# Layer 0 attention of a two-layer encoder: gate and reciprocal loads on POOL's queue, wider steps, a copied block of meta columns, and a shared PSUM bank read by ScalarE

## The chip, the cores and the metric

The kernel runs on one core of a Trainium2 chip. The core has TensorE (PE in the profile; PEld is its weight load), VectorE (DVE), ScalarE (ACT), GpSimd (POOL) and SyncE (SP), which issues most of the DMAs; POOL issues DMAs too. Each engine, and each queue of DMA issues, works in the order in which the program lists its instructions. The metric is the device time of one execution in microseconds (us), lower is better. Before the change it is 1822.5 us, the median of three runs (1821.57 to 1823.12).

## The reference

Two layers work on 512 tokens, with 16 learned meta tokens put in front, of width 2048. Layer 0 is softmax attention, layer 1 gated linear attention. Each layer is wrapped in two RMS norms and a residual. The change touches layer 0 and one helper that both layers use. What layer 0 computes:

```python
proj = h @ w_in                      # q 16 heads, k and v 8 heads of 128, gate 16 x 128
q = axial_rope(rmsnorm(q, q_norm)); k = axial_rope(rmsnorm(k, k_norm))
s = q @ k.T * 128 ** -0.5            # per head; two query heads share a k and a v
p = softmax(s)
o = p @ v
y = (o * silu(gate)) @ w_out
```

## The kernel before

All activations lie with features on the partitions and the 528 tokens along the free axis (512 real tokens, then the 16 meta tokens). Every product is made of three: each operand is split into a high part of fewer bits and the rest, and high x high, high x low and low x high are added in PSUM (`three`, lines 154 to 156; the weights' split is a cast on ACT, line 131, and a subtraction on DVE, line 132). A projection of 128 output features (`project`) is 2 halves x 16 blocks x 3 matmuls of 264 columns.

**How the order is made.** The text of the kernel is traced in the order of a small planner, `Clock`. It counts the time of projections (each triple of matmuls adds 3 x 271/2400 us) and lets generators take turns: a generator that yields 5.0 goes on when 5.0 us of projections have been laid down. The traced order is only a priority. The program's scheduler then lays out each engine's list, and may put an instruction of lower priority earlier, if it thinks the engine free and the operands ready. Weights are traced with a higher priority, so that their loads run ahead.

**Gates and values.** The gate projections of heads 0 to 12 and the v projections come first, in pairs of 128 features by a scheme of seven half-size products in place of eight (`seven`). Two outputs y1 and y2 are put together from partial sums. Some sums stay in PSUM: bank `p1` is read, and then the next product is added on top. Its third reading gave y2's right half, by an add on DVE straight from PSUM (line 249); two products later the bank is added to again. `seven` is called 18 times: 8 in layer 0's input, 4 in its output, 6 in layer 1's input. The gates lie in DRAM (`g_d`) until they are used.

**Attention.** The loop over the 8 groups (one k and v head, two query heads) runs three things at once. The three projections for the next group's k and q are PE's steady work. `attention` goes over 9 query tiles of the present group, one per step of `SLOTS` (2.9 us, 3.2 in the last group): scores in the one PSUM buffer `s` (two banks, lines 683 to 685), row maximum on DVE (688), exp with row sum on ACT (691), a second exp that writes the meta columns twice more into the tail of `pn` (693), the reciprocal of the row sum (695 or 697); half a step later the tile is transposed on PE (703, 705) and split (707 to 710), and the product with v follows (723 to 726). The next tile's scores can only start when line 693 has read `s`. At a group's end `inverses` stores the reciprocals of the row sums to DRAM (`r_d`).

`stored_gates` is the third: for the two heads of the group before, it loads the gates (line 655, SP's queue, buffers `gr`, two), loads a head's reciprocals as a row on all partitions (`inverse`, line 637, SP's queue, buffer `rb`, one), multiplies the gate by the first norm's factor (660, DVE), takes its SiLU (139 to 141 on ACT, the product 671 on POOL, buffers `gs`, two), multiplies by the reciprocals (`divided`, 642 for 512 and 643 for 16 columns, POOL), multiplies the head's output (665, DVE) and stores it by POOL's queue (666). Heads 13 to 15 have their gates projected in place (`gate`) in the last group. `rope` turns q and k: four DMAs (312) and three operations (313 to 315) on POOL, behind the evacuation of the projection (305, 306), while a sum of squares on PE (326, 327) gives the norm (329, 333).

Of the kernel before, what the change touches and what calls it, by code (L numbers as in the profile page):

```python
# [10 lines left out]
F32 = mybir.dt.float32  # L11
F32R = mybir.dt.float32r
I32 = mybir.dt.int32
AF = mybir.ActivationFunctionType
# [5 lines left out]
P = 128  # L20
# [12 lines left out]
G_HEADS = 4  # L33
SCALE = 128 ** -0.5
AHEAD = 400
SLOTS = (2.9,) * 7 + (3.2,)


class Clock:
# [43 lines left out]
def hybrid_encoder(  # L83
# [132 lines left out]
    def seven(src, c, ys, th, tl, free, ps_x):  # L216
# [58 lines left out]
        A.copy(y2[:, r], p5)  # L275
        sums(a11, a12, a11)
        product(parts(a21), of_t(T3), p1, True)
        add(y2[:, r], p1, y2[:, r])
        product(parts(a11), of_u(1, 1), p5, True)
        add(y1[:, r], p5, y1[:, r])  # L280
        product(parts(a22), of_t(T4), p1, True)
# [350 lines left out]
            rope(qw, sq, outs[i], (4.0, 8.8, 9.8))  # L632
        return qk, vv

    def inverse(h):
        rb = wa.tile([P, T], F32, tag="rb", name="rb", bufs=1)
        nc.sync.dma_start(out=rb, in_=r_d[h // 2, h % 2:h % 2 + 1, :].broadcast_to([P, T]))
        return rb

    def divided(gs, rb):  # L640
        by = gs[:, :SEQ].rearrange("p (t q) -> p t q", t=4)
# [9 lines left out]
    def stored_gates(hs, held):  # L651

        grs = [wa.tile([P, T], F32, tag="gr", name="gr") for _ in hs]
        for gr, h in zip(grs, hs):
            nc.sync.dma_start(out=gr, in_=g_d[h])
        yield 6.0
        for gr, h in zip(grs, hs):
            rb = inverse(h)
            yield 5.0
            V.tensor_tensor(gr, gr, rrow, op=ALU.mult)  # L660
            gs = silu(gr)
            divided(gs, rb)
            yield 4.0
            og = held[h % 2]
            V.tensor_tensor(og, og, gs, op=ALU.mult)
            nc.gpsimd.dma_start(out=og_d[h], in_=og)

    def silu(gr):
        gs = wa.tile([P, T], F32, tag="gs", name="gs", bufs=2)
# [10 lines left out]
    def softmax(n, qh, ql, kh, kl, inv):  # L680
        s = ps_s.tile([P, 2, 512], F32, tag="s", name="s")[:n, :, :HALF]
        for i, (a, b) in enumerate(HALVES):
            PE.matmul(s[:, i], qh, kh[:, a:b], start=True, stop=False)  # L683
            PE.matmul(s[:, i], ql, kh[:, a:b], start=False, stop=False)
            PE.matmul(s[:, i], qh, kl[:, a:b], start=False, stop=True)  # L685
        mx = wa.tile([P, 1], F32, tag="mx", name="mx")[:n]
        sm = wa.tile([P, 1], F32, tag="sm", name="sm")[:n]
        V.reduce_max(mx, s, axis=AX.XY, negate=True)  # L688
        pn = pn_bufs[n_pn[0] % NP][:n]
        n_pn[0] += 1  # L690
        A.activation(pn[:, :T].rearrange("p (a b) -> p a b", a=2), s, AF.Exp, bias=mx, accum_out=sm)  # L691
        tail = pn[:, SEQ:].rearrange("p (r m) -> p r m", r=3)
        A.activation(tail[:, 1:, :META], s[:, 1, HALF - META:].unsqueeze(1).broadcast_to([n, 2, META]), AF.Exp, bias=mx)  # L693
        if inv is None:
            V.reciprocal(tail[:, ::2, META], sm.broadcast_to([n, 2]))
        else:
            V.reciprocal(inv[:n], sm)
        return pn
# [36 lines left out]
    def attention(g, qk, vv, o_sb, slot):  # L735
        qh, ql, kh, kl = qk
        q0 = (0, Q1)
        last = g == KV - 1
        rs = None if last else wa.tile([P, 9], F32, tag="rs", name="rs")
        early, late = [[[None], [None]] for _ in range(2)]  # L740

        def tile_of(a, t):
            cell, end = (late, 272) if t > 1 else (early, 256)
            t2 = t % 2
            done = t2 and not (t > 1 and a == 0)
            return (P, q0[a] + t * P, [(cell[a], 0, t2 * P, P)], [(cell[a], 256 * (t > 1), end, a)] if done else [],
                    [] if t2 else [cell[a]], a * 4 + t)
        todo = [tile_of(0, t) for t in range(4)]
        todo.append((2 * META, SEQ, [(late[a], a * META, 256, META) for a in range(2)], [(late[0], 256, 272, 0)],
                     [late[1]], 8))  # L750
        first = tile_of(1, 2)
        todo += [first[:4] + ([],) + first[5:], tile_of(1, 3), tile_of(1, 0), tile_of(1, 1)]
        prev = None
        for item in todo + [None]:
            if item is not None:
                n, c, puts, ends, fresh, i = item
                pn = softmax(n, qh[:, c:c + n], ql[:, c:c + n], kh, kl, None if last else rs[:, i:i + 1])
            yield slot / 2
            if prev is not None:
                n_, _, puts_, ends_, fresh_, _ = prev[0]  # L760
                for cell in fresh_:
                    cell[0] = p_tiles()
                transposed(prev[1], n_, [(cell[0], qc, cc, m) for cell, qc, cc, m in puts_])
                for cell, cc, m, a in ends_:
                    clk.after(slot * 1.1, lambda cell=cell, cc=cc, m=m, a=a:
                              weighted(cell[0], cc, m, vv, o_sb[a], last))
            yield slot / 2
            prev = (item, pn) if item is not None else None
        if not last:
            inverses(g, rs)  # L770
        yield slot * 0.65

    def o_tiles():
        return [wa.tile([P, T], F32, tag="o", name="o_sb", bufs=4) for _ in range(2)]
# [3 lines left out]
    for g in range(KV):  # L778
# [8 lines left out]
        for h in gates:  # L787
            if h < 13:
                continue
            rb = inverse(h)  # L790
            gs = gate(h)
            divided(gs, rb)
            og = held[h % 2]
            V.tensor_tensor(og, og, gs, op=ALU.mult)
# [755 lines left out]
```

## Time and profile before

| | |
|---|---|
| median of 3 runs | 1822.5 us |
| the profiled execution | 1825.49 us, span 1823.7 |
| mean granted TensorE clock | 0.986 |
| PE busy | 1757.1 us, 96% of the span |
| DVE, ACT, POOL busy | 63%, 55%, 19% |
| layer 0's attention | 286 to 790 us of the span |
| DMA, mean | 120 GB/s |

The page's rows give line, engine, operation, and output and inputs by the program's names, then how often and how long. In a timeline the first number is the start in us from the span's start, the second the length; in brackets stands how long the engine had been idle and what it was waiting for. A line of waits names engine, tile and line that waited, then the releaser, the sum in us, how many times, and the longest. A row that has SPq shows SP's queue of DMA issues.

### The profile page before, as it was taken

Reading aid. Unit: us, or ns where it says so; the run is one execution under the profiler, and the core shown is the slowest. Engines: PE = TensorE matmul, PEld = TensorE weight load, DVE = VectorE, ACT = ScalarE, POOL = GpSimd, SP = SyncE. Lnnn points to the kernel's source line nnn. Section 1 sums busy time; section 2 is a strip of 40 time slices with the busy share of each in tenths; the row PEclk is TensorE's granted clock in tenths of the full one; section 3 lists DMA queues with packets and bytes.
Section 4 is the critical chain, followed back from the end, with each engine's and each line's share of the span. In section 5 each row is a group of like instructions: output and inputs, shape, how many; then the busy total and the mean of one; then the engine's idle time right before and its main releaser. Section 6 shows DMA issues by size and latency. Waiting matters only on the chain.

```text
span 1823.7 us, 31598 instructions
## 1 busy us (share of the span) xinstructions
PE 1757.1 (96%) x12427; PEld 1650.0 (90%) x12427; DVE 1152.8 (63%) x1805; ACT 997.5 (55%) x2038; POOL 347.0 (19%) x451
## 2 busy tenths in 40 slices
PE   8999999998998999999999999999999999999998
PEld 8999999898898999899999989988898988888886
DVE  5867766565565556586749686658585775764224
ACT  5534346555565556564447544458585775863221
POOL 3113102424433442223141101110010100000000
PEclk9999999999999999999999999999999999999999
DMA  8444434323333433364466344343342332354323
GB/s 255 144 124 118 128 117 135 92 74 95 95 88 89 109 87 85 97 201 134 126 215 199 117 122 129 99 126 100 86 114 74 104 101 74 106 156 167 99 93 128
DMA packets 274005, 218.83 MB, mean 120 GB/s; under 512 B 13084, under 2 KB 243168, under 8 KB 273328
## 3 DMA queue, kind: packets, MB, share of 16 engines
q1 hardware_dynamic: 256976, 164.71, 31.9%
q0 software_dynamic: 16880, 52.10, 8.4%
q8 instruction: 98, 1.61, 0.4%
q14 instruction: 51, 0.42, 0.1%
HBM read 176.83 MB, written 33.44 MB: 115 GB/s over the span
## 4 chain that ended last, share of the span: by engine, by line
PE 62%; issue 15%; POOL 6%; DMA 6%; DVE 5%; ACT 5%; SPq 0%; DVEq 0%; POOLq 0%; ACTq 0%
PE pp L154 10%; PE pp L156 10%; PE pp L155 10%; PE f L1462 2%; PE f L1460 2%; PE f L1461 2%; PE pp L240 2%; PE pp L241 2%; PE pp L242 2%; DVE wlo L132 2%; PE px L242 2%; PE px L240 2%; PE px L241 2%; ACT whi L131 2%; DMA wraw<-in_attn_w_in_dram 1%
## 5 line engine op out<-in xcount | busy, mean ns | idle before, releaser
L154 PE MATMUL pp<-uh,whi 128*128 128x264 f32 (+1 forms) x1872 | 588.3, 314 | 1.2 <-ACT y L869 0.8
L156 PE MATMUL pp<-uh,wlo 128*128 128x264 f32 (+1 forms) x1872 | 579.1, 309 | 1.6 <-DVE wlo L132 1.2
L155 PE MATMUL pp<-ul,whi 128*128 128x264 f32 (+1 forms) x1872 | 578.8, 309 | 1.3 <-DVE ul L444 1.3
L132 DVE TENSOR_TENSOR wlo<-wraw,whi 128x1024 fp32r<-128x1024 f32 (+1 forms) x226 | 275.6, 1220 | 252.4 <-ACT whi L131 252.0
L156 PEld LDWEIGHTS pp<-uh,wlo 128*128 128x128 f32 x1872 | 356.6, 190 | 19.1 <-DVE wlo L132 1.7
L154 PEld LDWEIGHTS pp<-uh,whi 128*128 128x128 f32 x1872 | 356.4, 190 | 18.1 <-ACT y L869 1.0
L131 ACT CAST whi<-wraw 128x1024 fp32r<-128x1024 f32 (+1 forms) x226 | 235.1, 1041 | 248.8 <-PE f L1462 83.4
L155 PEld LDWEIGHTS pp<-ul,whi 128*128 128x128 f32 x1872 | 356.5, 190 | 15.3 <-DVE ul L444 1.9
L131 ACT CAST whi<-x 128x1024 fp32r<-128x1024 f32 x72 | 75.5, 1049 | 106.9 <-PE pp L241 55.7
L132 DVE TENSOR_TENSOR wlo<-x,whi 128x1024 fp32r<-128x1024 f32 x72 | 92.6, 1287 | 41.0 <-ACT whi L131 40.9
L691 ACT ACTIVATE pn<-s,mx 128x528 f32<-128x528 f32 (+1 forms) x72 | 50.3, 698 | 65.4 <-DVE mx L688 64.7
L240 PE MATMUL px<-uh,whi 128*128 128x264 f32 x288 | 82.2, 285 | 1.4 <-ACT whi L131 1.4
L242 PE MATMUL px<-uh,wlo 128*128 128x264 f32 x288 | 82.3, 286 | 1.3 <-DVE wlo L132 1.2
L241 PE MATMUL px<-ul,whi 128*128 128x264 f32 x288 | 81.5, 283 | 0.0
L312 POOL DMA_DIRECT2D qs<-qw x96 | 47.9, 504 | 167.4 <-ACT sq L306 144.0
L1462 PE MATMUL f<-whi,ul 128*128 128x512 f32 x192 | 75.6, 394 | 0.0
L1460 PE MATMUL f<-whi,uh 128*128 128x512 f32 x192 | 75.5, 393 | 0.0
L683 PE MATMUL s<-kh,qh 128*128 128x264 f32 (+1 forms) x144 | 44.6, 310 | 32.0 <-ACT pn L693 32.0
L1461 PE MATMUL f<-wlo,uh 128*128 128x512 f32 x192 | 75.3, 392 | 0.0
L688 DVE TENSOR_REDUCE mx<-s 128x1 f32<-128x528 f32 (+1 forms) x72 | 50.7, 705 | 21.7 <-PE s L685 20.8
L708 DVE TENSOR_TENSOR pl<-pT,ph 128x512 fp32r<-128x512 f32 (+1 forms) x80 | 47.6, 595 | 26.2 <-ACT ph L707 25.0
L240 PE MATMUL pp<-t0h,whi 128*128 128x264 f32 x192 | 55.6, 290 | 3.8 <-DVE y L249 3.7
(482 smaller groups left out, 4434.5 us busy)
## 6 DMA issues: line engine op xcount, KB each, us to landing
wraw<-in_gla_w_in_dram SPq DMA_DIRECT2D x82, 512.0 KB, 3.9
wraw<-in_attn_w_in_dram SPq DMA_DIRECT2D x75, 512.0 KB, 4.5
wraw<-in_gla_w_out_dram SPq DMA_DIRECT2D x32, 512.0 KB, 3.9
wraw<-in_attn_w_out_dram SPq DMA_DIRECT2D x23, 512.0 KB, 4.5
x<-in_attn_w_in_dram SPq DMA_DIRECT2D x19, 512.0 KB, 4.4
x<-in_gla_w_in_dram SPq DMA_DIRECT2D x14, 512.0 KB, 4.5
qs<-qw POOLq DMA_DIRECT2D x96, 66.0 KB, 4.0
g_d<-y POOLq DMA_DIRECT2D x20, 264.0 KB, 2.4
```

Source lines behind the costliest of these rows:

```text
L131: A.copy(hi, src)
L132: V.tensor_tensor(lo, src, hi.bitcast(F32), op=ALU.subtract)
L154: PE.matmul(ps, wh, uh[:, k, a:b], start=first, stop=False)
L155: PE.matmul(ps, wh, ul[:, k, a:b], start=False, stop=False)
L156: PE.matmul(ps, wl, uh[:, k, a:b], start=False, stop=last)
L240: PE.matmul(ps, w[0][:, k], bh[:, k], start=k == 0 and not more, stop=False, skip_group_check=more)
L241: PE.matmul(ps, w[0][:, k], bl[:, k], start=False, stop=False, skip_group_check=more)
L242: PE.matmul(ps, w[1][:, k], bh[:, k], start=False, stop=k == KH - 1, skip_group_check=more)
L688: V.reduce_max(mx, s, axis=AX.XY, negate=True)
L1460: PE.matmul(ps, uh[:, k, ts], wh[:, kk], start=(k == 0), stop=False)
L1461: PE.matmul(ps, uh[:, k, ts], wl[:, kk], start=False, stop=False)
L1462: PE.matmul(ps, ul[:, k, ts], wh[:, kk], start=False, stop=(k == KT - 1))
```

## The change

- `SLOTS` goes from 2.9 to 3.3 us per tile, and from 3.2 to 3.5 in the last group. The last yield of `attention` is dropped in all groups but the last.
- The gates are loaded by POOL's queue. The reciprocals are too, and into the gate's own buffer, once its SiLU is made; the tile `rb` is gone. `stored_gates` makes both SiLUs first, and has other yields.
- For head 13 the load of the reciprocals comes after its gate, into a buffer of the tag `gr`.
- The tail of `pn` is filled by a copy of its meta columns from SBUF, in place of a second exp from PSUM.
- In `seven`, ACT copies `p1` into y2's left half, which is free until the end, and DVE adds it to the right half from there.

```diff
-SLOTS = (2.9,) * 7 + (3.2,)
+SLOTS = (3.3,) * 7 + (3.5,)
...
         product(parts(a21), of_t(T3), p1, True)
-        add(y2[:, r], p1, y2[:, r])
+        A.copy(y2[:, l], p1)
+        add(y2[:, r], y2[:, l], y2[:, r])
         product(parts(a11), of_u(1, 1), p5, True)
...
-    def inverse(h):
-        rb = wa.tile([P, T], F32, tag="rb", name="rb", bufs=1)
-        nc.sync.dma_start(out=rb, in_=r_d[h // 2, h % 2:h % 2 + 1, :].broadcast_to([P, T]))
-        return rb
+    def inverse(h, rb):
+        nc.gpsimd.dma_start(out=rb, in_=r_d[h // 2, h % 2:h % 2 + 1, :].broadcast_to([P, T]))
...
         for gr, h in zip(grs, hs):
-            nc.sync.dma_start(out=gr, in_=g_d[h])
-        yield 6.0
+            nc.gpsimd.dma_start(out=gr, in_=g_d[h])
+        yield 8.0
+        gss = []
         for gr, h in zip(grs, hs):
-            rb = inverse(h)
+            V.tensor_tensor(gr, gr, rrow, op=ALU.mult)
+            gss.append(silu(gr))
+            inverse(h, gr)
             yield 5.0
-            V.tensor_tensor(gr, gr, rrow, op=ALU.mult)
-            gs = silu(gr)
-            divided(gs, rb)
-            yield 4.0
+        for gr, gs, h in zip(grs, gss, hs):
+            divided(gs, gr)
+            yield 3.0
             og = held[h % 2]
             V.tensor_tensor(og, og, gs, op=ALU.mult)
             nc.gpsimd.dma_start(out=og_d[h], in_=og)
+            yield 2.0
...
-        A.activation(tail[:, 1:, :META], s[:, 1, HALF - META:].unsqueeze(1).broadcast_to([n, 2, META]), AF.Exp, bias=mx)
+        A.copy(tail[:, 1:, :META], pn[:, SEQ:T].unsqueeze(1).broadcast_to([n, 2, META]))
...
             inverses(g, rs)
-        yield slot * 0.65
+        yield slot * 0.65 if last else 0.0
...
-            rb = inverse(h)
             gs = gate(h)
+            rb = wa.tile([P, T], F32, tag="gr", name="rb")
+            inverse(h, rb)
             divided(gs, rb)
```

## The prediction

> **What bounds the kernel now.** I read the page first, then the stages, then who waits for whom. Line 1 of the page:
>
> ```profile
> span 1823.7 us, 31598 instructions
> PE 1757.1 (96%) x12427; PEld 1650.0 (90%) x12427; DVE 1152.8 (63%) x1805; ACT 997.5 (55%) x2038; POOL 347.0 (19%) x451
> ```
>
> TensorE is the bound: 66.6 us of the span are without a matmul. Busy time by stretch (length; then PE, PEld, DVE, ACT, POOL busy; clock granted; DMA share; GB/s) puts most of that into layer 0's attention, 286 to 790 us:
>
> ```profile
> 286.00:790.00 504.00, 465.74 (x3665) 455.73 (x3664) 296.16 (x556) 299.06 (x738) 181.02 (x211) 0.96 0.34 96
> 338.00:402.00 64.00, 57.16 (x441) 55.83 (x440) 37.19 (x68) 36.79 (x90) 23.00 (x28) 0.95 0.33 93
> 360.00:368.00 8.00, 7.92 (x54) 7.73 (x53) 3.30 (x7) 2.73 (x7) 2.93 (x3) 0.79 0.12 34
> 374.00:380.00 6.00, 6.00 (x41) 5.92 (x40) 3.12 (x8) 4.13 (x13) 2.50 (x5) 0.74 0.64 178
> 658.00:722.00 64.00, 61.49 (x505) 60.35 (x504) 37.03 (x73) 37.51 (x97) 26.00 (x30) 1.00 0.33 89
> ```
>
> There 504.0 - 465.7 = 38.3 us are idle, and the clock is down as well. A group of two heads takes about 64 us; the one in the second row loses 6.8 us idle and 5% of its clock. PE's own waits, and in the timeline the first and last of two kinds:
>
> ```profile
> PE s L683 <- ACT pn L693: 32.0, 12, 3.9
> PE pp L240 <- DVE y L249: 4.1, 2, 3.7
> ...
> 358.79 0.39 PE L683 MATMUL s<-kh,qh 128*128 128x264 f32 x1 [3.74 <-ACT pn L693]
> ...
> 681.47 0.39 PE L683 MATMUL s<-kh,qh 128*128 128x264 f32 x1 [2.28 <-ACT pn L693]
> ```
>
> ```profile
> 373.55 0.48 PE L683 MATMUL s<-kh,qh 128*128 128x264 f32 x1 [2.68 <-ACT pn L693]
> ...
> 570.17 0.39 PE L683 MATMUL s<-kh,qh 128*128 128x264 f32 x1 [2.70 <-ACT pn L693]
> ```
>
> 32.0 us go to one thing: the scores of the next tile need the only PSUM buffer `s`, which the second exp of the tile before (L693) releases last. The waits are regular. The second kind comes four times, 2.7 us each: 10.8. The other 21.2 are the first kind: six waits, from 3.74 us in group 1 to 2.28 in group 6, and two small ones. Each wait of 2.68 or more is followed by a slow clock: 8 us at 0.79 is 1.68 us lost, 6 us at 0.74 is 1.56; I take 1.6. The wait of 2.28 has no such cost, its stretch stands at 1.00. Nine long waits (five and four) make 14.4 us. The whole prize in this stage is 21.2 + 10.8 + 14.4 = 46.4 us.
>
> L693 is only the last step of a chain that came late. What came before it in the first kind, on POOL, then DVE, then ACT:
>
> ```profile
> 350.42 1.57 POOL L642 TENSOR_TENSOR gs<-gs,rb 128x512 f32<-128x512 f32 x1 [4.09 <-DMA rb<-r_d]
> 351.90 0.59 POOL L666 DMA_DIRECT2D og_d<-o_sb  x1
> 352.48 1.97 POOL L312 DMA_DIRECT2D qs<-qw  x4
> 354.47 0.23 POOL L643 TENSOR_TENSOR gs<-gs,rb 128x16 f32<-128x16 f32 x1
> ```
> ```profile
> 350.67 0.43 DVE L329 SCALAR_TENSOR_TENSOR sq<-ssq,erow 128x264 f32<-128x264 f32 x1 [0.48 <-PE ssq L327]
> 354.74 1.79 DVE L665 TENSOR_TENSOR o_sb<-o_sb,gs 128x528 f32<-128x528 f32 x1 [3.64 <-POOL gs L643]
> 356.45 0.69 DVE L688 TENSOR_REDUCE mx<-s 128x1 f32<-128x528 f32 x1
> ```
> ```profile
> 356.56 0.64 ACT L139 ACTIVATE gs<-gr 128x528 f32<-128x528 f32 x1 [5.22 <-DVE o_sb L665]
> ...
> 357.79 0.68 ACT L691 ACTIVATE pn<-s,mx 128x528 f32<-128x528 f32 x1
> ```
>
> The second head's reciprocals `rb` have one buffer, so their load starts when the first head's division is done. POOL waits 4.09 us for it, then issues a store and four rope DMAs before the last 16 columns (L643). DVE stands 3.64 us at L665, with the row maximum (L688) queued behind; ACT stands 5.22 us behind DVE. In the second kind a gate load is late:
>
> ```profile
> 355.98 7.40 SPq L655 DMA_DIRECT2D gr<-g_d  x2
> ...
> 365.90 0.71 DVE L660 TENSOR_TENSOR gr<-gr,rrow 128x528 f32<-128x528 f32 x1 [3.68 <-DMA gr<-g_d]
> ```
> ```profile
> SPq L655 <- POOL gs L671: 69.6, 11, 8.0
> DVE o_sb L665 <- POOL gs L643: 26.1, 13, 3.8
> DVE gr L660 <- DMA gr<-g_d: 16.9, 7, 4.1
> ```
>
> SP holds the load until POOL has read the old gate in the same buffer (69.6 us over 11 loads); DVE stands 3.68 us at L660 for it, and the next maximum, exp and scores come that much later.
>
> **The change, part by part.** The sum starts from the profiled execution, 1825.5 us (1.8 around the span), 3.0 above the median of 1822.5; 3.0 comes off at the end.
>
> *Reciprocals.* They now go into each head's own gate buffer, after both SiLUs, by POOL's queue; `rb` and its one-buffer wait are gone. The prices:
>
> ```profile
> rb<-r_d SPq DMA_DIRECT2D x14, 264.0 KB, 3.9
> gr<-g_d SPq DMA_DIRECT2D x13, 264.0 KB, 2.8
> ...
> gr<-kq_d POOLq DMA_DIRECT2D x1, 256.0 KB, 3.1
> ```
> ```profile
> L642 POOL TENSOR_TENSOR gs<-gs,rb 128x512 f32<-128x512 f32 x14 | 22.5, 1607 | 58.4 <-DMA rb<-r_d 58.4
> ...
> L643 POOL TENSOR_TENSOR gs<-gs,rb 128x16 f32<-128x16 f32 x14 | 3.2, 228 | 0.1
> ```
> ```profile
> 341.23 5.46 SPq L637 DMA_DIRECT2D rb<-r_d  x2
> L1378 POOL DMA_DIRECT2D gr<-kq_d x1: 536/536/536, 1295.2 to 1295.2; - x1
> ```
>
> In the group shown the first reciprocals could be issued at 341.23. Two POOL issues of 0.54 and 3.9 to landing end at 346.2; two divisions of 1.61 + 0.23 end at 349.9, where L643 now ends at 354.7. DVE arrives at L665 when L329 is done, 351.1. So the wait goes with 1.2 us to spare, if POOL does nothing else between. The load now holds POOL until the store of the reciprocals has landed, as it held SP before 341.23; behind it on POOL stand the divisions, the stores of gated heads and the rope, and who waits for these is DVE at L665 and the next group's q.
>
> *Gate loads.* They wait no more for the SiLU's product but for the division in their buffer: 349.9, two issues of 0.54, 3.1 to landing make 354.1, where DVE now gets its tile at 365.9. The SP queue loses 27 issues and the weights behind them are freed; PE waits for no weights there, so that is worth nothing. POOL gains 27 x 0.54 = 14.5 us, about 2.1 a group; it was busy 181 of 504 us and idle 58.4 before L642 alone, which covers it. Without cover it would be 14.5 us on the rope chain, or nothing, since rope is early.
>
> How much goes cannot be read off, as the program's scheduler lays the order on each engine and steps are only priorities. Bounds: all 46.4 us, or nothing (below nothing: third rival). I take two thirds, 30.9: both causes are taken away by name, but with 1.2 us to spare for the first kind a single store or rope issue of POOL's in the wrong place brings some of it back.
>
> *Meta columns.* An exp from PSUM becomes a copy in SBUF:
>
> ```profile
> L693 ACT ACTIVATE pn<-s,mx x72: 262/279/290, 296.6 to 780.2; 128x32 f32<-128x32 f32 x64, 32x32 f32<-32x32 f32 x8
> ```
>
> The same ACT time, but `s` is free 0.28 us earlier. *Wider steps* put 0.4 us more projection (planner's time) between two tiles. Together 0.68 us off each wait that stays: four of twelve, 2.7 us. On the planner's clock the last tile's transposes now come at 3.0 + 9.5 x 3.3 = 34.4, past the 32.5 us of a group's three projections (96 x 3 matmuls of 271/2400 us), so no projection lies between them and the group's end. Its scores stand at 3.0 + 8 x 3.3 = 29.4, with 3.1 us of projection behind them, as much as a tile has anywhere; the dropped last step lets the next group's projection follow at once. I take 0.
>
> *Pairs.* The shared bank is read by ACT instead of DVE, 18 times. The long wait there:
>
> ```profile
> 158.21 2.31 DVE L132 TENSOR_TENSOR wlo<-x,whi 128x1024 fp32r<-128x1024 f32 x1
> 160.44 0.42 DVE L249 TENSOR_TENSOR y<-pp,y 128x264 f32<-128x264 f32 x1
> ```
> ```profile
> 160.91 0.39 PE L240 MATMUL pp<-t0h,whi 128*128 128x264 f32 x1 [3.69 <-DVE y L249]
> L275 ACT COPY y<-px x18: 356/372/378, 131.3 to 1186.5; 128x264 f32<-128x264 f32 x18
> ```
>
> The third matmul of that product needs `wlo`, ready at 160.52: a free bank gains 0.4 us, not 3.7. A copy of 0.37 us has a product of 24 matmuls as cover, behind it on ACT stand casts of weights, and the add on DVE, now from SBUF, leaves the path; if ACT is held there, one wait of 3.7 and its clock (5.3) is the worst. I take 0.
>
> *Last group.* Head 13's reciprocals are loaded after its gate. Early as now it costs nothing, late it costs issue, landing and clock, 0.5 + 3.9 + 1.6 = 6 us. I take 0, for a freed gate buffer is there long before.
>
> Sum: 1825.5 - 30.9 - 2.7 = 1791.9, less 3.0: **1789 us**. All waits gone gives about 1774; half of them kept and the worst of the pairs about 1804.
>
> **The rivals.** *The loads' queue is worth nothing.* Only step and copy act: 12 x 0.68 = 8.2 us, and the four waits of 2.7 fall to 2.0, under the 2.28 that left the clock alone: 4 x 1.6 = 6.4. 1825.5 - 14.6 - 3.0 = 1808. For it: DVE still meets POOL at L665; against: SP's 69.6 us. The Trainium skill ("DMA: Bandwidth & Descriptors", Issuing engines are not separate DMA queues) says that issuing from more engines only saves the sequencer's issue time, usually small; by that rule this rival holds. The trace shows a queue's wait that it doesn't count.
>
> *No change.* The scheduler keeps DVE's order, and POOL's 2.1 us a group put L643 as late as before: 1822. For it: in group 1 the rope's four issues already came between L642 and L643.
>
> *Slower: a gate load caught behind a rope on POOL.* The queue stands long before each rope:
>
> ```profile
> 374.31 2.01 POOL L312 DMA_DIRECT2D qs<-qw  x4 [11.30 <-ACT sq L306]
> ```
>
> A load queued behind it comes 11.3 us late, and DVE stands in L660. DVE's 3.68 cost PE 2.68, so 11.3 cost 10.3 and 1.6 of clock: 11.9, in six groups 71.4, less the 46.4 saved: +25, 1847. It decides from a hold of 7.1 us a group (46.4 / 6 - 1.6 + 1.0). Against it: 349.9 lies ahead of that rope.
>
> **How the numbers follow.** Forecast 0.58, no queue gain 0.12, no change 0.10, slower 0.20. About 0.2% (3.6 us) is what a measurement of this kernel can tell from no change. Faster: 0.58 + 0.12 = 0.70; same 0.10; slower 0.20. The forecast's own range is 1774 to 1804; 8 in 10 need the second and third case and the near half of the slower one: 1772 to 1832.
>
> **What would show it.** Right: PE's wait on `s` well under 15 us, the release now on L691; DVE's waits at L665 and L660 under 1 us each; the clock of the attention stretch at 0.98 or more; the wait at the pair's bank moved to `wlo`, not gone. Wrong: DVE stands for POOL or a gate load at another place as long as before, or the scores wait on a rope. If the waits go and the time does not, the price of a wait was wrong.

## The result and the profile after

| | before | after |
|---|---|---|
| median | 1822.03 us (4 runs, 1819.18 to 1823.12) | 1808.25 us (4 runs, 1804.63 to 1811.06) |
| profiled execution | 1825.49 us, span 1823.7 | 1808.31 us, span 1806.5 |
| mean granted clock | 0.986 | 0.993 |

The ratio is 0.9926, with a 95% interval of 0.9904 to 0.9947: faster by 13.8 us, where 33 were forecast. The direction held. 1808 lies inside the range of 8 in 10 (1772 to 1832) and outside the forecast's own (1774 to 1804), and the gain is less than half of what was forecast. In the changed kernel the lines stand 1 to 3 further down: the scores are L685 to L687, the maximum L690, the exp L693, the division L641 and L642, the gate's load L654, its product with `rrow` L658, the gated product L666.

Four landmarks in both timelines divide the gain. The first scores start 2.8 us earlier (293.3 to 290.5), the last ones of layer 0 12.1 (776.5 to 764.4), layer 1's gates 14.4 (1198.7 to 1184.3), the last output matmul 17.4 (1814.6 to 1797.2). So 9.3 us came from the attention itself, for which the forecast had 33.6 (30.9 and 2.7).

The changed kernel's page, line 1, and its attention stretch in the windows:

```profile
span 1806.5 us, 31569 instructions
PE 1750.5 (97%) x12427; PEld 1641.0 (91%) x12427; DVE 1148.5 (64%) x1805; ACT 1005.5 (56%) x2056; POOL 361.8 (20%) x478
```
```profile
286.00:790.00 504.00, 472.19 (x3743) 459.01 (x3743) 297.89 (x569) 308.08 (x750) 200.34 (x245) 0.98 0.36 101
```

PE is busy for 472.2 us of this stretch in place of 465.7, at a clock of 0.98 in place of 0.96 (the stretch of time is the same, and the attention now ends 12 us sooner in it). Who waits there, PE first, then DVE:

```profile
PE s L685 <- ACT pn L693: 19.2, 8, 3.7
```
```profile
DVE o_sb L666 <- POOL gs L642: 45.8, 13, 7.5
DVE gr L658 <- DMA gr<-g_d: 15.6, 13, 1.9
```

The wait on the scores' bank fell from 32.0 us in 12 to 19.2 in 8, and is now released by the first exp: the meta copy does what it says. But DVE stands longer for the division than before, 45.8 us where it was 26.1. The forecast had this wait gone. One group on POOL and then on DVE shows it:

```profile
343.53 0.59 POOL L637 DMA_DIRECT2D gr<-r_d  x1 [8.95 <-DMA r_d<-rs]
344.11 1.98 POOL L313 DMA_DIRECT2D qs<-qw  x4
346.08 0.57 POOL L637 DMA_DIRECT2D gr<-r_d  x1
348.17 1.54 POOL L641 TENSOR_TENSOR gs<-gs,gr 128x512 f32<-128x512 f32 x1 [1.52 <-DMA gr<-r_d]
349.67 0.22 POOL L642 TENSOR_TENSOR gs<-gs,gr 128x16 f32<-128x16 f32 x1
350.19 0.58 POOL L654 DMA_DIRECT2D gr<-g_d  x1 [0.30 <-POOL gs L642]
...
354.73 1.34 POOL L316 TENSOR_TENSOR qw<-qw,qs 128x528 f32<-128x528 f32 x1
356.02 1.59 POOL L641 TENSOR_TENSOR gs<-gs,gr 128x512 f32<-128x512 f32 x1
```
```profile
349.92 0.71 DVE L666 TENSOR_TENSOR o_sb<-o_sb,gs 128x528 f32<-128x528 f32 x1 [2.97 <-POOL gs L642]
350.55 0.70 DVE L690 TENSOR_REDUCE mx<-s 128x1 f32<-128x528 f32 x1
...
357.82 0.71 DVE L666 TENSOR_TENSOR o_sb<-o_sb,gs 128x528 f32<-128x528 f32 x1 [2.73 <-POOL gs L642]
358.44 0.70 DVE L690 TENSOR_REDUCE mx<-s 128x1 f32<-128x528 f32 x1
```

The rope's four DMA issues lie between the two loads of reciprocals, and its three products between the two divisions, so the second division starts at 356.02. The forecast had both done at 349.9, "if POOL does nothing else between". DVE stands twice a group, in the first six groups for 2.5 to 5.4 us and then for 2.6 to 4.4; before the change it was 0.3 to 1.1 and then 3.2 to 3.8. Both times the next row maximum is queued right behind the gated product. PE feels the second stand most: the scores for the maximum at 358.44 were ready at 353.7, and the scores after them have to wait:

```profile
360.02 0.59 PE L685 MATMUL s<-kh,qh 128*128 128x264 f32 x1 [2.04 <-ACT pn L693]
```

Of PE's 19.2 us, 14.0 in six waits follow a second stand, and 5.3 in two follow a first one.

### The profile page after: what moved, and what is told of

Read it like the earlier page. It is cut to its first block, busy times and chain, and to the rows that moved or that the text cites. A ratio compares the mean times of both kernels' runs of the same rounds, so it can differ in the third digit from the quotient of the medians.

```text
span 1806.5 us, 31569 instructions
## 1 busy us (share of the span) xinstructions
PE 1750.5 (97%) x12427; PEld 1641.0 (91%) x12427; DVE 1148.5 (64%) x1805; ACT 1005.5 (56%) x2056; POOL 361.8 (20%) x478
## 5 line engine op out<-in xcount | busy, mean ns | idle before, releaser
L154 PEld LDWEIGHTS pp<-uh,whi 128*128 128x128 f32 x1872 | 355.4, 190 | 17.3 <-POOL whi L383 1.3
L132 DVE TENSOR_TENSOR wlo<-x,whi 128x1024 fp32r<-128x1024 f32 x72 | 93.4, 1302 | 41.7 <-ACT whi L131 41.5
L693 ACT ACTIVATE pn<-s,mx 128x528 f32<-128x528 f32 (+1 forms) x72 | 50.2, 698 | 62.5 <-DVE mx L690 62.4
L690 DVE TENSOR_REDUCE mx<-s 128x1 f32<-128x528 f32 (+1 forms) x72 | 50.7, 704 | 29.0 <-PE s L687 28.4
L710 DVE TENSOR_TENSOR pl<-pT,ph 128x512 fp32r<-128x512 f32 (+1 forms) x80 | 47.7, 596 | 25.6 <-ACT ph L709 25.0
L685 PE MATMUL s<-kh,qh 128*128 128x264 f32 (+1 forms) x144 | 43.5, 302 | 19.2 <-ACT pn L693 19.2
L242 PE MATMUL pp<-t0h,wlo 128*128 128x264 f32 x192 | 54.5, 284 | 1.2 <-DVE wlo L132 1.2
```

Source lines behind the costliest of these rows:

```text
L132: V.tensor_tensor(lo, src, hi.bitcast(F32), op=ALU.subtract)
L154: PE.matmul(ps, wh, uh[:, k, a:b], start=first, stop=False)
L242: PE.matmul(ps, w[1][:, k], bh[:, k], start=False, stop=k == KH - 1, skip_group_check=more)
```

## The experiments

The theory after the result was that the loads' part works and something else in the change takes half of it back; the rivals were that POOL's queue is the harm, that the loads' part is worth little, or that POOL's order in the changed kernel is. The parts come first, each by itself. Names of lines are those of each kernel; the medians of before differ by up to 2.6 us between the five sets of runs, so kernels of different sets are compared by their ratios to before.

### Each part alone

**Steps alone.** `SLOTS` of the change and the dropped last yield, on the kernel before:

```diff
-SLOTS = (2.9,) * 7 + (3.2,)
+SLOTS = (3.3,) * 7 + (3.5,)
-        yield slot * 0.65
+        yield slot * 0.65 if last else 0.0
```

> Only the wider steps and the dropped last step, on the kernel before. Theory A (the gain of the whole change is from steps, copy and pairs; the moved loads give nothing, since DVE still stands for POOL in two places a group): 5 to 8 us faster than before, near 1815, with PE's waits on the scores' buffer shorter but still one or two a group. Rival B (the moved loads carry the gain, as the prediction had it): 0 to 3 us faster, waits as before.

Measured 1830.53 us, ratio 1.0039 (1.0027 to 1.0051): slower by 7 us. PE's waits and DVE's in this kernel:

```profile
PE s L683 <- ACT pn L693: 38.6, 15, 5.4
```
```profile
DVE o_sb L665 <- POOL gs L643: 45.6, 13, 5.2
```

The 32.0 and 26.1 us of before have become 38.6 and 45.6. The 45.6 is nearly the 45.8 of the changed kernel: DVE's longer stand comes with the steps.

**Meta copy alone.**

```diff
-        A.activation(tail[:, 1:, :META], s[:, 1, HALF - META:]..., AF.Exp, bias=mx)
+        A.copy(tail[:, 1:, :META], pn[:, SEQ:T]...)
```

> Only the copy of the meta columns in place of the second exp, on the kernel before. Both theories: the scores' buffer comes free 0.28 us earlier, 12 waits, so 2 to 4 us faster, near 1819. If the waits of 2.7 us fall under the point where the clock drops, up to 8 us.

Measured 1824.91 us, ratio 1.0 (0.9988 to 1.0011). PE's wait on `s` is 29.7 us in place of 32.0, and the time does not move.

**Loads alone.** POOL's queue, the gate's own buffer for the reciprocals, both SiLUs first, with the yields that belong to this; steps, meta columns and pairs as before:

```diff
+    def inverse(h, rb):
+        nc.gpsimd.dma_start(out=rb, in_=r_d[...])
...
-            nc.sync.dma_start(out=gr, in_=g_d[h])
+            nc.gpsimd.dma_start(out=gr, in_=g_d[h])
...
+            gss.append(silu(gr))
+            inverse(h, gr)
```

> Only the gate and reciprocal loads on POOL's queue, with the new order of SiLUs and divisions, on the kernel before. Theory A: within 3 us of before (1819 to 1825). Rival B: 10 us faster or more (1812 or less), PE's waits on the scores' buffer half of 32 us.

Measured 1800.14 us, ratio 0.987 (0.9855 to 0.9884): 24 us faster, more than the whole change. POOL and DVE in the group that was shown above:

```profile
342.17 1.12 POOL L636 DMA_DIRECT2D gr<-r_d  x2 [3.20 <-DMA r_d<-rs]
345.90 1.57 POOL L640 TENSOR_TENSOR gs<-gs,gr 128x512 f32<-128x512 f32 x1 [2.61 <-DMA gr<-r_d]
...
350.05 0.70 POOL L641 TENSOR_TENSOR gs<-gs,gr 128x16 f32<-128x16 f32 x1
...
352.16 1.00 POOL L312 DMA_DIRECT2D qs<-qw  x2
```
```profile
347.68 0.71 DVE L665 TENSOR_TENSOR o_sb<-o_sb,gs 128x528 f32<-128x528 f32 x1 [1.94 <-POOL gs L641]
...
354.18 0.70 DVE L665 TENSOR_TENSOR o_sb<-o_sb,gs 128x528 f32<-128x528 f32 x1
...
356.93 0.71 DVE L689 TENSOR_REDUCE mx<-s 128x1 f32<-128x528 f32 x1 [0.43 <-PE s L686]
```

Here it runs as forecast: two loads in a row, both divisions done at 350.75 (349.9 were worked out), the rope after them. The second gated product waits for nothing, and the next maximum waits for PE's scores and not PE for it. What PE waits for in this stretch now is the sum of squares of the rope, whose operands DVE and ACT split:

```profile
PE ssq L327 <- DVE sl L132: 8.4, 7, 1.5
PE ssq L326 <- ACT sh L131: 7.8, 6, 2.2
```

**Pairs alone.**

```diff
-        add(y2[:, r], p1, y2[:, r])
+        A.copy(y2[:, l], p1)
+        add(y2[:, r], y2[:, l], y2[:, r])
```

> Only the shared bank of the pairs copied by ScalarE, on the kernel before. Theory A: 4 to 5 us faster, 1817 to 1818, the wait of 3.7 us at the bank gone. Rival B, as the prediction had it (the product needs its low weights anyway): within 1 us of before.

Measured 1820.33 us, ratio 0.9988 (0.9976 to 0.9999): about 2 us, just apart from none. The forecast had the wait of 3.69 moved to `wlo`; it is gone, in this kernel and in the changed one. DVE in the changed kernel:

```profile
155.37 4.62 DVE L132 TENSOR_TENSOR wlo<-x,whi 128x1024 fp32r<-128x1024 f32 x2
159.91 1.55 DVE L249 TENSOR_TENSOR y<-y 128x264 f32<-128x264 f32 x1
```

The split of the weights stands ahead of the add, as before, and PE waits 0.16 us for `wlo`. `wlo` is earlier too: the sums of weights (L233) that make its operand start 1.8 us sooner in the changed kernel and 0.6 with the pairs alone, and the second of them takes 1.23 us in place of 2.23. How much of the 3.69 us is the bank is therefore not shown.

### The loads' part taken apart

**All parts but the steps.** The changed kernel with `SLOTS` and the last yield of before.

> The changed kernel with the old steps and the old last step (so loads, copy and pairs). Theory C (the wider steps bring the store of the reciprocals so near to the next rope that the scheduler lays the rope's work on POOL between the two heads' loads and divisions, and DVE stands for that): 8 to 12 us faster than the changed kernel, 1796 to 1800, POOL's two divisions next to each other, no long wait on the scores' buffer. Rival D (copy and pairs cost what is missing): it stays near 1808.

Measured 1793.1 us, ratio 0.9846 (0.9833 to 0.9859). The changed kernel differs from this one by the steps alone and stands at 0.9926: the steps cost 0.8%, 15 us. PE's wait on `s` is down to 1.0 us. DVE's stand for the division in this kernel:

```profile
DVE o_sb L666 <- POOL gs L642: 5.3, 7, 1.6
```

**The loads on SP's queue.** The loads' part alone, as above, with both loads issued by SP:

```diff
-        nc.gpsimd.dma_start(out=rb, in_=r_d[...])
+        nc.sync.dma_start(out=rb, in_=r_d[...])
...
-            nc.gpsimd.dma_start(out=gr, in_=g_d[h])
+            nc.sync.dma_start(out=gr, in_=g_d[h])
```

> The run with only the loads changed, but both loads on SP's queue as before: what is left is the reciprocals' own buffer and the order of the SiLUs. If the buffer does it (the skill's rule, a queue saves only issue time): within 3 us of that run, 1797 to 1803. If the queue does it: 1810 or more, with gate loads late behind SP's waits.

Measured 1789.43 us, ratio 0.9834 (0.982 to 0.9847), against 0.987 (0.9855 to 0.9884) with POOL's queue: SP's is better by 0.36%, 6.6 us. The gain does not come from the queue that the change names.

**Own buffer, old order.** The same on SP's queue, but each head finished before the next one's SiLU, as in the kernel before:

```diff
-        gss = []
...
-            gss.append(silu(gr))
+            gs = silu(gr)
             inverse(h, gr)
             yield 5.0
-        for gr, gs, h in zip(grs, gss, hs):
             divided(gs, gr)
-            yield 3.0
+            yield 4.0
```

> Kernel before with the reciprocals loaded by SP's queue into the gate's own buffer, each head done by itself as before (SiLU, load, division, then the second head), so without the new order of the two SiLUs. With the new order this gave 1789.4. Theory B (the one buffer of the reciprocals was the cause): 1788 to 1794, order worth nothing. Theory R (the order lets the second head's SiLU and load run ahead of the first division): 1803 to 1815, with the second head's division waited for at the gated product.

Measured 1793.18 us, ratio 0.9852 (0.9832 to 0.9871), which overlaps with the 0.9834 of the new order. So 27 of the 30 us come with the gate's own buffer for the reciprocals, in place of the one buffer `rb` (with it their load moves behind the head's SiLU, and a yield of 2.0 is added); the order of the SiLUs is worth 0 to 3.

**All but the steps, on SP's queue.**

> Everything of the change but the steps and the queue: own buffers, SiLUs first, copy and pairs, with both loads on SP's queue. The runs so far add up (SP's queue 11 us better than POOL's, copy and pairs 7 us): 1780 to 1788. If the parts don't add: 1789 to 1793, the level of the two runs it is made of.

Measured 1789.84 us, ratio 0.982 (0.9807 to 0.9833). This and the loads' part on SP's queue alone are the best kernels found, 18 us below the changed one; pairs and copy add nothing that can be measured on top. The attention stretch of this kernel:

```profile
286.00:790.00 504.00, 485.42 (x3945) 474.74 (x3944) 328.48 (x602) 318.11 (x770) 199.95 (x224) 1.00 0.38 111
```

PE is busy 485.4 us of 504 at a full clock. Of the 38.3 idle us of before 18.6 are left.

### Why the steps harm

**The last yield alone.** The changed kernel with the old `SLOTS`, the last yield still dropped.

> The changed kernel with the old steps of 2.9 and 3.2, but the last step dropped. Theory G (the chain from the store of the reciprocals to the gated output must fit between the last tile of a group and the first of the next; wide steps cut the projection work between them from 9.3 to 6.1 us of the planner, and the stretch from store to next row maximum from 18 to 11 us): the work between is 9.3 as before, so within 4 us of the run without steps, 1790 to 1797. Rival I (the dropped last step is the harm): 1804 or more.

Measured 1794.64 us, ratio 0.985 (0.9837 to 0.9863), as without both. The harm is the step's size.

**POOL's order.** In the changed kernel, priority for the loads of reciprocals and the divisions:

```diff
+            with tc.high_priority(AHEAD):
+                inverse(h, gr)
...
+            with tc.high_priority(AHEAD):
+                divided(gs, gr)
```

> The changed kernel, steps kept, with the loads of the reciprocals and the divisions at a higher priority, so that both loads come first on POOL and the second division ahead of the rope's products. Theory C: most of the loss of the steps comes back, 1798 to 1803. Rival F (the steps cost by themselves, because the last tile's work lies past the projections): it stays within 3 us of 1808.

Measured 1812.33 us, ratio 0.9959 (0.9947 to 0.9971): no gain, so the theory behind this run fell. The order did come right, POOL first, then DVE:

```profile
408.23 1.12 POOL L637 DMA_DIRECT2D gr<-r_d  x2 [7.79 <-DMA r_d<-rs]
...
415.74 1.56 POOL L641 TENSOR_TENSOR gs<-gs,gr 128x512 f32<-128x512 f32 x1
```
```profile
414.79 0.71 DVE L668 TENSOR_TENSOR o_sb<-o_sb,gs 128x528 f32<-128x528 f32 x1 [3.05 <-POOL gs L642]
415.41 0.70 DVE L692 TENSOR_REDUCE mx<-s 128x1 f32<-128x528 f32 x1
...
417.52 1.59 DVE L668 TENSOR_TENSOR o_sb<-o_sb,gs 128x528 f32<-128x528 f32 x1 [1.40 <-POOL gs L642]
```

The loads are together and the divisions are no longer parted by the rope's products, yet DVE comes to the gated product 3.05 us early, with the next maximum behind it. The second stand is down to 1.40 us, but PE still waits 25.0 us on `s`: the second maximum (424.11 in this group) now stands behind the next gate's product (L658) and q's product with its norm (L334), and these wait 1.56 us for the gate's load and 1.35 for the rope, which POOL does later than before. So a new wait took the place of the old one, and the run does not show that POOL's order was harmless.

**The gated product on POOL**, so that DVE cannot stand for it:

```diff
-            V.tensor_tensor(og, og, gs, op=ALU.mult)
+            G.tensor_tensor(og, og, gs, op=ALU.mult)
```

> The changed kernel, steps kept, with the product of the head's output and its gate moved from DVE to POOL, so that DVE has no instruction that waits for POOL's division. Theory C (the cost is DVE's stand): PE's 19 us of waits on the scores' buffer mostly go, 1796 to 1802, although POOL's order is as it was. Rival F: within 3 us of 1808.

Measured 1827.72 us, ratio 1.0038 (1.0026 to 1.005). Inconclusive on the steps, since a new wait took the old one's place: POOL's chain is longer, the gate loads queued on POOL come later, and DVE stands 44.4 us at L658 for them.

**Tiles started later.** The changed kernel with 6.2 instead of 3.0 us of projections ahead of a group's first tile:

```diff
-        att = clk.drive(chain(iter([3.0]), attention(...)))
+        att = clk.drive(chain(iter([6.2]), attention(...)))
```

> The changed kernel, wide steps kept, with each group's tiles started 6.2 instead of 3.0 us into its projections, so that the work between two groups is 9.3 again. Theory G: 6 to 14 us faster than the changed kernel, 1794 to 1802, although the last tiles lie still further past the projections. Rival F (wide steps cost by themselves, since the last tiles have no projections beside them): 1808 or slower.

Measured 1820.7 us, ratio 1.0 (0.9988 to 1.0012): another miss. PE waits 34.6 us on `s`, and DVE stands 5.0 to 5.9 us at the first gated product of each group.

**Tiles started earlier**, 0.0 in that place, on the kernel with all parts but the steps.

> The run without steps (1793), with each group's tiles started at 0.0 instead of 3.0 us, so that the work between two groups is 6.3 as with the wide steps. Theory G: 8 to 15 us slower than that run, 1801 to 1808, DVE standing about 3 us for POOL's divisions again. Rival F: within 3 us of 1793 or faster.

Measured 1834.93 us, ratio 1.0084 (1.0055 to 1.0112). This says nothing on the steps: the scores now come before the rope has made their q, and PE waits 41.5 us for `qh`.

**A step between.** The changed kernel with 3.1 us (3.4 in the last group) in place of 3.3 (3.5).

> The changed kernel with a step of 3.1 instead of 3.3 us (3.4 instead of 3.5 in the last group), and nothing else. The wider step cost 15 us on top of the other parts. On the planner's clock a group's last transposes stand at 3.0 + 9.5 x 3.1 = 32.45, just inside the 32.5 us of the three projections, where 3.3 puts them at 34.4. Theory P (harm comes from the last tile lying past the projections, with no matmuls left to cover it): with 3.1 the harm is gone, 1792 to 1797, and PE's waits on the scores' bank under 8 us. Theory S (each 0.2 us of step takes 1.9 us of cover from the end of each group, in proportion): half the harm, 1799 to 1803, waits of 8 to 14 us. Theory J (what the scheduler makes of any change is chance): anywhere.

Measured 1817.62 us, ratio 0.998 (0.9968 to 0.9993): worse than 3.3, so neither the end of the projections nor a loss in proportion to the step explains it; that it is chance what the scheduler makes of a change is not excluded. The wait moves to another place. PE, then DVE:

```profile
PE o L726 <- DVE pl L710: 34.0, 7, 6.1
```
```profile
DVE o_sb L666 <- POOL gs L642: 24.1, 7, 4.4
```

Behind the gated product on DVE there now stands not a maximum but a split of weights, then q's, and then the low part of a transposed tile (L710), and PE waits for that before the weighted sum, 5 us a group.

**Steps with SP's queue.** The changed kernel, both loads issued by SP.

> The changed kernel, steps of 3.3 kept, with the gates and reciprocals loaded by SP's queue. Theory O (the wide steps harm because they let the rope's DMAs and products come between POOL's loads and divisions, so that a load is issued late): with the loads off POOL the harm is gone, 1789 to 1796. Theory E (they harm because the next group's first tiles find DVE waiting for the division, whoever loads): the 10 us that SP's queue gains stay, the 15 us stay too, 1798 to 1806, with PE's waits on the scores' bank at 15 us or more.

Measured 1809.25 us, ratio 0.9939 (0.9918 to 0.996). The harm does not depend on the queue; what SP's queue gains is lost as well. POOL now makes the two divisions in a row, without the rope between, and PE still waits 16.2 us on `s`: DVE reaches the second product right behind the first, 10.1 us after the reciprocals' store in the first group, where the second division is done at 12.3, and the first maximum stands behind both.

**A narrower step**, 2.6 us, on the best kernel.

> All parts with SP's queue and a step of 2.6 instead of 2.9 us (1789.8 with 2.9). The last transposes stand at 3.0 + 9.5 x 2.6 = 27.7, so 4.8 us of projections follow a group's tiles in place of 1.9. Theory E (cover between the last tile and the next group's first tiles is what counts): no wait of DVE at the gated product, 1783 to 1790. Rival (tiles packed closer than their own chain of maximum, exp and transposes): new waits on the scores' bank inside the group, 1795 to 1815. If neither wait is there, 1788 to 1792: nothing is left to gain from the step.

Measured 1804.7 us, ratio 0.9902 (0.9883 to 0.9921), 15 us worse than 2.9. POOL and DVE in the first group, and DVE's sum:

```profile
340.10 0.22 POOL L642 TENSOR_TENSOR gs<-gs,gr 128x16 f32<-128x16 f32 x1
```
```profile
340.35 2.00 DVE L666 TENSOR_TENSOR o_sb<-o_sb,gs 128x528 f32<-128x528 f32 x1 [6.09 <-POOL gs L642]
```
```profile
DVE o_sb L666 <- POOL gs L642: 39.9, 7, 6.1
```

The division starts as early as ever (338.59, 6.5 us after the reciprocals' store at 332.05; in the best kernel 341.80, 6.4 after 335.42); DVE is 6.09 us too early for it. PE's wait on `s` stays at 2.5 us, and what it waits for is the weighted sum's operands, 15.8 us.

**The gated product later.** The next theory: a step harms only through the place that it gives the gated product in DVE's fixed order. To move the product alone, both divisions come first and 10 us of projections (planner's time) before the products, once on the changed kernel and once on the narrow one:

```diff
-        for gr, gs, h in zip(grs, gss, hs):
+        for gr, gs in zip(grs, gss):
             divided(gs, gr)
-            yield 3.0
+        yield 10.0
+        for gs, h in zip(gss, hs):
             og = held[h % 2]
...
-            yield 2.0
+            yield 1.0
```

> The changed kernel, steps of 3.3 and POOL's queue kept, with both divisions ahead and then 10 us of projections (planner's time) before the two gated products. Theory D (a step is harmful only through the place that it gives the gated product in DVE's fixed order: DVE stood 45.8 us there with 3.3, 24.1 with 3.1, 39.9 with 2.6, 4 to 8 with 2.9): with the product placed behind the divisions DVE stands under 8 us there, PE's wait on the scores' bank falls under 8 us, and the 15 us that the steps cost come back, 1791 to 1799. Theory E (wide steps leave too little cover behind the tiles whatever stands on DVE): waits stay at another place, 1803 to 1815.

> The same late product on the version with a step of 2.6 and SP's queue (1804.7), which otherwise has DVE standing 39.9 us for the division, 5 to 6 us at each group's first product. Theory D: that wait falls under 8 us and PE's wait on the weighted sum's operands (15.8 us) with it, 1786 to 1794. Theory E says that a narrow step has the cover already and its harm is tiles packed too close: 1800 to 1808, with the wait on the weighted sum kept.

Measured 1822.43 us, ratio 0.9996 (0.9981 to 1.001), and 1803.31 us, ratio 0.9892 (0.9874 to 0.991). Both miss, but not as a verdict on the theory: the first product did not move. DVE's stand in the first kernel, and in the second:

```profile
DVE o_sb L667 <- POOL gs L642: 61.0, 13, 8.0
```
```profile
DVE o_sb L667 <- POOL gs L642: 40.8, 7, 6.3
```

DVE reached the first product 7.4 us after the reciprocals' store in the first of these kernels, and 2.2 in the second, to the tenth as without the edit; the second product DVE reached even earlier in the first kernel, 12.5 to 15.5 us after the store in place of 14.4 to 17.3. Here a yield did not set an instruction's place on its engine, and the theory stayed untested.

**What the traces of all these runs have in common.** Measured from the store of the reciprocals (L645, SP's queue) in the first six groups of each kernel: when the load of them is issued, which waits for the store to land; when the first division is done; when DVE arrives at the product; and what the DMA moves in the 4 us behind the store.

| kernel | step | load issued | division done | DVE arrives | GB/s | ratio |
|---|---|---|---|---|---|---|
| all but the steps, SP | 2.9 | +1.6 to 3.0 | +7.5 to 8.2 | +7.3 | 1 to 18 | 0.982 |
| all but the steps | 2.9 | +1.8 to 3.1 | +7.5 to 8.9 | +7.3 | 1 to 25 | 0.9846 |
| after | 3.3 | +3.8 to 5.3 | +9.9 to 12.8 | +7.4 | 132 to 138 | 0.9926 |
| steps with SP's queue | 3.3 | +3.7 to 5.3 | +9.7 to 11.6 | +7.4 | 132 to 138 | 0.9939 |
| steps alone | 3.3 | +3.7 to 5.0 | +10.3 to 10.9 | +7.4 | 132 to 136 | 1.0039 |
| step between | 3.1 | +1.8 to 3.6 | +8.3 to 10.2 | +5.9 | 1 to 26 | 0.998 |
| narrower step | 2.6 | +2.1 to 3.1 | +7.5 to 8.3 | +2.2 | 14 to 38 | 0.9902 |

With 3.3 DVE arrives when it does with 2.9; the division is 2 to 4 us later, because the store lands 2 us later and the load takes longer as well. SP's queue in the changed kernel, and in the one with all but the steps:

```profile
339.13 0.37 SPq L149 DMA_DIRECT2D wraw<-in_attn_w_in_dram  x1
339.55 0.57 SPq L645 DMA_DIRECT2D r_d<-rs  x1
```
```profile
335.90 0.37 SPq L645 DMA_DIRECT2D r_d<-rs  x1
...
341.82 0.37 SPq L149 DMA_DIRECT2D wraw<-in_attn_w_in_dram  x1
```

With 3.3 a load of weights (128 x 1024 f32, 0.52 MB) is issued 0.42 us ahead of the store; the 132 GB/s in 4 us are that load. In the changed kernel the store lands 0.16 to 0.18 us behind these weights in every group (3.70 us after its issue, the weights 3.53, in the first), and in the others of 3.3 us 0.2 to 1.0 behind them. With 2.9 the next weights come 5.9 us or more behind the store, when the reciprocals are nearly there. From issue to landing (the last number, a median) of the reciprocals' load and of their store, in the DMA issues of the changed kernel and then of the one with all but the steps:

```profile
gr<-r_d POOLq DMA_DIRECT2D x13, 264.0 KB, 4.8
...
r_d<-rs SPq DMA_DIRECT2D x7, 4.0 KB, 3.7
```
```profile
gr<-r_d POOLq DMA_DIRECT2D x13, 264.0 KB, 3.8
...
r_d<-rs SPq DMA_DIRECT2D x7, 4.0 KB, 2.2
```

So the wide step moves the end of a group to just behind a load of weights, and the round trip of the reciprocals through DRAM shares the DMA with it. This holds in the kernels of 3.3 us that differ in queue, priority and order (the changed one, SP's queue, POOL's order, product on POOL, product later), and with the steps alone. In the late start it is 185 to 190 GB/s in those 4 us, and the store lands as late there, 4.2 to 4.7 us after its issue. With 3.1 the weights come 2.96 us behind the store, on top of the load (4.9 to landing), and DVE arrives at 5.9. With 2.6 the DMA is free and the division early, but DVE arrives 5 us sooner. Only 2.9, of the four sizes, has the weights out of the way and DVE in time.

This accounts for the first stand of a group: with store and load as quick as with 2.9, the first division would be done about when DVE arrives (7.5 to 8.9 against 7.4). The second stand, which PE feels most, has the rope on POOL before it too, and one more thing differs in the same kernels. The next group's first scores end 9.6 us behind the store in every kernel with 3.3 but the late start, and 14 to 18 us behind it in those with 2.9, the loads' part and the old start (13.2 to 13.8 in the kernel before). With 2.9 both divisions are done before those scores, at 12.3 us at the latest; with 3.3 both are done after them. The late start was to bring this distance back and did not: it is 10.5 us there. So two causes stand side by side, the store behind the weights and the next scores' nearness to the store.

That the weights delay the store is read from these traces, in which they are issued 0.42 us ahead of it in kernel after kernel. What that delay is worth of the 15 us is not shown; a run that changes only the order, the store ahead of the weights with the wide step kept, was not made.

## Why the prediction was partly right

**What bounds the kernel: right.** The one buffer `rb` and its consequences were the prize; with them gone PE's wait on `s` is 1.9 us in the best kernel, and the clock of the stretch 1.00.

**Reciprocals and gate loads: right in mechanism and nearly in size, wrong in the name.** Forecast were 30.9 us; all parts but the steps gave 28 (0.9846), the loads alone 24 with POOL's queue and 30 with SP's. The 30.9 were two thirds of the whole, a share that was chosen and not worked out, so that they came near is partly luck. The condition "if POOL does nothing else between" holds there and fails in the changed kernel. The prediction laid weight on SP's wait of 69.6 us. The Trainium skill ("DMA: Bandwidth & Descriptors", Issuing engines are not separate DMA queues) says that more issuing engines save only issue time. The runs agree with it as against the prediction: POOL's queue gains nothing over SP's here and costs 6.6 us (0.987 against 0.9834).

**Meta copy: too high.** The release moved to the first exp as read, but 0 us came of it.

**Wider steps: the step that failed.** "I take 0", plus 0.4 us off each wait that stays. They cost 7 us alone and 15 on top of the rest. The argument looked at projections as cover for PE and asked where they lie behind the last tile. It did not ask how the chain from the store of the reciprocals to the gated products then lies against the next group's first tiles. The store had no term in the sum, and "PE waits for no weights there" was the only word on the weights. The two divisions that the forecast had worked out to be done at 349.9 start with that store: in the changed kernel the first is done at 349.9 and the second at 357.8, and DVE stands 45.8 us for them where the forecast had the wait gone. That the wide step is the cost is shown by the runs with and without it (1830.5 alone; 1793.1 without it, 1794.6 with the dropped yield kept). The traces show the store behind a load of weights, the first division 2 to 4 us later, the rope between the two heads on POOL, and the next scores nearer to the store; which of these makes how much of the 15 us stays open.

**Pairs: forecast 0, about 2 us gained.** The wait went instead of moving to `wlo`, which was earlier too.

**The rivals.** "The loads' queue is worth nothing" gave 1808, which is what was measured, but by another mechanism, so the agreement is chance: it took the gain from step and copy, which gave a loss and nothing. Its title is true of the queue and false of the loads' part. "A gate load caught behind a rope" did not come about: gate loads cost DVE 15.6 us in 13 waits, 1.9 at most. Of the signs named, the clock of 0.98 and the release by the first exp held; the wait on `s` under 15 us and DVE's waits under 1 us did not, and "DVE stands for POOL at another place as long as before" was what showed. The forecast's lower end, about 1774, takes off all waits (46.4 us) and also the 2.7 us of the waits that stay; with the waits alone it is 1776.

**Open** is whether the wide step with the store put ahead of the weights comes to the 1793 us of the other parts or below, why the scheduler has DVE arrive at 2.2 us with a step of 2.6 and at 5.9 with 3.1, and how the 15 us divide between the late store, the rope that lies ahead of the second division, and the next scores' coming sooner after the store.

## What to carry to other kernels

A single buffer between a load and an in-order engine is worth looking for first: here it was 27 us, and giving it a second place to land was enough, whichever queue loads it. When a planner's step size is changed, look at what each in-order queue then holds at the places where a group ends, and how soon the next group comes: here the wider step put a 0.52 MB load of weights ahead of a small store whose round trip the next group waits for, brought the next scores nearer to that store, and took back half of the gain. And when a change of several parts falls short, run each part alone and all but one: the part that was priced at zero was the one that mattered.

## What was unexpected of the hardware

**Waits and the clock.** In the prediction each wait of PE of 2.68 us or more was followed by a slow clock. In the changed kernel that is not so regular. Its PE timeline, then the windows behind these two waits:

```profile
668.71 0.39 PE L685 MATMUL s<-kh,qh 128*128 128x264 f32 x1 [3.01 <-ACT pn L693]
...
726.16 0.59 PE L685 MATMUL s<-kh,qh 128*128 128x264 f32 x1 [3.73 <-ACT pn L693]
```
```profile
669.00:677.00 8.00, 6.79 (x54) 6.16 (x54) 6.43 (x12) 5.89 (x16) 2.75 (x5) 1.00 0.43 131
...
727.00:735.00 8.00, 8.00 (x49) 7.99 (x49) 4.50 (x9) 4.41 (x10) 3.00 (x3) 0.69 0.28 68
```

After 3.01 us the clock stays at 1.00 (and for the 16 us behind), after 3.73 it falls to 0.69, which is 2.5 us lost in 8. Nor is a short wait safe: after the wait of 2.04 us at 360.02 the clock is 0.86 from 361 to 369, so the rival's reckoning that waits of 2.0 us cost no clock does not hold. By these rows the length of a wait alone does not decide.

**DVE beside POOL.** The same gated product (two inputs in SBUF) takes 0.71 us alone and 2.00 while POOL runs a division (the row at 340.35 above, with a division on POOL from 340.28); the add of the pairs took 0.42 us from PSUM before and 1.55 from SBUF now, both times with a product of the rope running on POOL. In both slow cases DVE's instruction ends shortly behind POOL's (342.35 after the division's 341.80, 161.46 after the product's 161.18), as if it had been held until POOL was through.
